# Hybrid decoder layer, last chunk of the input projection: twelve of its sums moved from VectorE to accumulating transfers, whole-weight units removed, and the end of the attention reordered

## The chip, the cores and the metric

The kernel runs on one core of one Trainium2 chip. The metric is the device time of one execution in microseconds (us); lower is better. The core has a matrix engine (TensorE, PE in the profile; PEld is its weight load), VectorE (DVE), ScalarE (ACT), GpSimd (POOL) and SyncE (SP). Each of them works through its own instructions strictly in the order in which the program wrote them, and waits on semaphores where an operand is not ready. Transfers are issued by SP (here: all large weight loads) or by POOL (here: small loads, spills, and whatever adds to its destination), and run on the core's 16 DMA engines, which all queues share.

## What is computed

One decoder layer for one sequence of 256 tokens and 2048 features, in float32. The part that matters:

```python
mod = (c_act @ w_mod + b_mod)[:, None, :]
sh_m, sc_m, g_m, sh_f, sc_f, g_f = jnp.split(mod, 6, axis=-1)
h = rmsnorm(x, mix_pre_w) * (1 + sc_m) + sh_m
proj = h @ w_in
cb, cc, cx, q, k, v, r, a_lr = jnp.split(proj, splits, axis=-1)
y_conv = cb * causal_dwconv3(cc * cx, conv_w)
...
o = gla_chunked(q, k, v, log_a)
o = rmsnorm(o, gla_norm_w) * jax.nn.silu(r)
x = x + g_m * rmsnorm(jnp.concatenate([y_conv, y_gla], -1) @ w_out, mix_post_w)
...
```

`w_in` has 6160 columns: cb, cc and cx with 1024 each, q and k with 512 each, v and r with 1024 each, and 16 for the gate. A second half (the ConvFFN, `w_up` and `w_down`) follows and is not touched.

## The kernel before, in words

**Products in three terms.** A float32 weight tile is loaded by SP, rounded by ScalarE to the faster format (`high`, L139, tile `wh`), and the remainder is formed by VectorE (`low`, L144, tile `wl`). The activations are split likewise. Each 128x128 weight block then takes three matmuls of 256 columns (L574, L575, L576). There are three buffers each for `wh` and `wl`, six for raw weights. A unit that is "plain" (L571) skips rounding and remainder and multiplies the whole float32 weights and activations; each such product shows as two matmul records.

**Chunks.** The modulation vectors are needed before `h` exists, so the 16 blocks of 128 features of `h` are made in four chunks of 2, 4, 5 and 5 blocks (`CHUNKS`), and the input projection runs once over its 48 column tiles for each chunk. The partial sums of a chunk are added into `proj[...]` tiles in SBUF by `evac` (L445 to L457): the first chunk's are copied by ScalarE, each later one added by VectorE (L457, 128x512, one for each pair of column tiles). The last chunk is the subject here. It has 18 units (below: u0 to u17), each of two or three column tiles: u0 to u5 make q, k and v; u6 to u14 make cc, cx and cb in turns; u15 to u17 make r. `FULL = (5, 9, 13)` (L46) makes u5, u9 and u13 plain, of two, three and two column tiles with five blocks each, so 35 products.

**What runs beside it.** The gated linear attention runs between those units: gate (gla_gate0 to 4), then nine levels of score blocks (`gla_level`), each with a difference on VectorE (diff), exponentials on ScalarE (decay), products on VectorE (mult), matmuls (products, L673) and a masked write into the score tile (put; from level 4 on a copy on ScalarE). `gla_v` turns v on TensorE (L662). `gla_out` ends it: `outputs` (L775 to L778) in u15, `norms` (eight squares on ScalarE, L386, a square root, L787, and a reciprocal on VectorE, L788) late in u15, `scaled` (eight scalings on ScalarE, L797) early in u16, then `turn` (L805) and `gate` for the four heads, the first turn late in u17. The convolution runs in four pairs of tiles (`conv_pair`, CONV = u9, u12, u13, u15): c0 is a product on VectorE (L600) and two scalings on ScalarE (L602), c1 in the next unit four fused operations and a product on VectorE (L135, L609) and a rounding on ScalarE (L611), c2 a remainder on VectorE (L615). Two more modulation vectors are summed meanwhile on VectorE, one 128x2048 row block for each step (`macc`, L135). Each such sum starts with a memset and a bias load, both on POOL (L177, L178); the one named f1 below starts early in u8 and is used by VectorE in the same step.

After u17 come the 16 units of the output projection (u18 and on, L841 to L843, matmuls of 512 columns), and then the ConvFFN.

**The order of the work** is written out by hand. `drive` (L74) walks the units; for unit i it emits, in this order: its `early` list, the load and rounding of unit i+2 (`prep`), the remainder of unit i+1 (`low`), its `pre` list, its matmuls, its `mid` list, the `fin` of unit i-1 (that is `evac`), and its `late` list. Each engine's queue is this order, cut down to its own instructions. `hf` tiles (three buffers, `hf_tile`, L420) hold modulated activations; in the last chunk a plain unit reads them until its matmuls are done.

Of the kernel before, what the change touches and what calls it, by code (L numbers as in the profile page):

```python
# [11 lines left out]
ALU = mybir.AluOpType  # L12
# [12 lines left out]
CHUNKS = (2, 4, 5, 5)  # L25
# [16 lines left out]
MODS = (10, 22, 32, 48, 68)  # L42
CHUNK1 = 12
BUSY_TAIL = (15, 16, 17)
F2_AT = (68, 73, 16)
FULL = (5, 9, 13)  # L46
FULL1 = ()
FULL2 = ()
NRAW = 6
# [17 lines left out]
def spread(steps, units):  # L67

    places = [p for u in units for p in (u.early, u.mid)]
    for i, f in enumerate(steps):  # L70
        places[i * len(places) // len(steps)].append(f)
# [31 lines left out]
def layer_kernel(ctx: ExitStack, tc, x, c, w_mod, b_mod, mix_pre_w, mix_post_w, w_in, conv_w, gate_w2, gate_b,  # L103
                 gla_norm_w, w_out, ffn_pre_w, ffn_post_w, w_up, ffn_conv_w, w_down, ident_in, masks_in, out):
    nc = tc.nc
# [12 lines left out]
    def nm(s):  # L118
        uid[0] += 1
        return f"{s}_{uid[0]}"  # L120

    def slot(shape, dt=F32):
        return big.tile(shape, dt, tag="big", name=nm("big"))

    def bank(shape):
        return psp.tile(shape, F32, tag="ps", name=nm("ps"))
# [7 lines left out]
    def stt(o, a, s, b, op0=ALU.mult, op1=ALU.add):  # L134
        nc.vector.scalar_tensor_tensor(o, a, s, b, op0=op0, op1=op1)  # L135
# [24 lines left out]
    def mod_steps(s0, n, a, w, nj, lag=0):  # L160

        accs, cur, rows = [], {}, []

        def use(j, r):
            stt(cur["acc"], r, c_act[:, j:j + 1], cur["acc"])

        def step(j):
            if j >= KT:  # L170
                use(*rows.pop(0))
                return
            if j == 0:
                acc = cur["acc"] = (slot([P, n, w]) if n * w <= 1024 else
                                    wts.tile([P, n, w], F32, tag="macc", name=nm("macc"), bufs=2))
                accs.extend(acc[:, s, :] for s in range(n))
                nc.gpsimd.memset(acc, 0.0)  # L177
                nc.gpsimd.dma_start(acc[0:1, :, :], b_mod_v[:, s0:s0 + n, a:a + w])  # L178
            m = nj if j < KT - nj or nj < 4 else 2
            if j % m == 0:  # L180
                cur["r"] = raw_tile([P, m, n, w])
                if m == 1:
                    nc.sync.dma_start(cur["r"][:, 0, :, :], w_mod_v[:, j, s0:s0 + n, a:a + w])
                else:
                    for s in range(n):
                        nc.sync.dma_start(cur["r"][:, :, s, :], w_mod_v[:, j:j + m, s0 + s, a:a + w])
            rows.append((j, cur["r"][:, j % m, :, :]))
            if j >= lag:
                use(*rows.pop(0))

        return accs, [lambda j=j: step(j) for j in range(KT + lag)]
# [192 lines left out]
    def square_sum(src, dst):  # L384
        jk = wts.tile([P, 512], BF16, tag="junk", name=nm("junk"), bufs=1)
        nc.scalar.activation(jk[:, :src.shape[-1]], src, AF.Square, accum_out=dst)  # L386
# [30 lines left out]
    def act_low(d, src):  # L417
        nc.vector.tensor_sub(d[:, :, 1, :], src, d[:, :, 0, :].bitcast(F32))

    def hf_tile():  # L420
        return wts.tile([P, 2, T], F32, tag="hf", name=nm("hf"), bufs=NHF)
# [23 lines left out]
    def evac(ci, pair, ps):  # L445

        name = names[pair // 2]
        if name not in proj:
            proj[name] = slot([P, 4, T])
        dst = proj[name][:, (pair % 2) * 2:(pair % 2) * 2 + 2, :]  # L450
        if pair not in written:
            written.add(pair)
            nc.scalar.activation(dst, ps, AF.Copy, scale=QS if name == "q" else 1.0)
        elif name == "q":
            stt(dst, ps, QS, dst)
        else:
            nc.vector.tensor_add(dst, dst, ps)  # L457

# [57 lines left out]
    def in_units(ci):  # L516
# [16 lines left out]
        def unit(tiles, plain, by_parts=False):  # L533
# [47 lines left out]
            def fin():  # L581
                for p in dict.fromkeys(nt // 2 for nt in tiles):
                    done[p] = done.get(p, 0) + sum(nt // 2 == p for nt in tiles)
                    if done[p] == 2 and p not in keep:
                        evac(ci, p, banks[p])

            return Unit(prep, lows, mm, [fin])

        return [unit(g, i in (PLAIN, FULL1, FULL2, FULL)[ci], ci == 0 and i == 0) for i, g in enumerate(groups)]

# [169 lines left out]
    def gla_out():  # L760

        st = {}

        def outputs():
            v, s = gla["v"], gla["s"]
            st["ss"] = small.tile([P, 2 * HEADS], F32, tag="gss", name="gss")
            st["ps"] = []
            for t in range(2):
                for g in range(2):
                    ps = bank([P, 2, 256])  # L770
                    for i in range(2):
                        h = g * 2 + i
                        hs = slice(h * 256, (h + 1) * 256)
                        if t == 0:
                            nc.tensor.matmul(ps[:, i, :], s[0][:, h, :], v[0][:, hs], start=True, stop=True)  # L775
                        else:
                            nc.tensor.matmul(ps[:, i, :], s[1][:, h, :], v[0][:, hs], start=True, stop=False)
                            nc.tensor.matmul(ps[:, i, :], s[2][:, h, :], v[1][:, hs], start=False, stop=True)  # L778
                    st["ps"].append(ps)

        def norms():
            ss = st["ss"]
            for t in range(2):
                for h in range(HEADS):
                    square_sum(st["ps"][2 * t + h // 2][:, h % 2, :], ss[:, t * 4 + h:t * 4 + h + 1])
            rs = small.tile([P, 2 * HEADS], F32, tag="grs", name="grs")
            nc.scalar.activation(rs, ss, AF.Sqrt, bias=eps_t, scale=1.0 / 256)  # L787
            nc.vector.reciprocal(rs, rs)  # L788
            st["rs"] = rs

        def scaled():
            rs = st["rs"]
            st["o"] = []
            for t in range(2):
                o = slot([P, 4, 256])
                for h in range(HEADS):
                    nc.scalar.activation(o[:, h, :], st["ps"][2 * t + h // 2][:, h % 2, :], AF.Copy,  # L797
                                         scale=rs[:, t * 4 + h:t * 4 + h + 1])
                st["o"].append(o)

        def turn(e2):
            st[e2] = ps = bank([P, 2, T])
            for i in range(2):
                for t in range(2):
                    nc.tensor.transpose(ps[:, i, t * P:(t + 1) * P], st["o"][t][:, e2, i * P:(i + 1) * P], ident)  # L805

        def gate(e2):
            r = proj[f"r{e2 // 2}"][:, (e2 % 2) * 2:(e2 % 2) * 2 + 2, :]
            for i in range(2):
                stt(r[:, i, :], st[e2][:, i, :], sv[:, 56 + i:57 + i], r[:, i, :], ALU.mult, ALU.mult)  # L810
            mts[4 + e2] = slot([P, 2, 2, T], F32R)
            nc.scalar.copy(mts[4 + e2][:, :, 0, :], r)

        def gate_low(e2):
            r = proj[f"r{e2 // 2}"][:, (e2 % 2) * 2:(e2 % 2) * 2 + 2, :]
            act_low(mts[4 + e2], r)

        return outputs, norms, scaled, turn, gate, gate_low

    def gate_silu(g):  # L820
# [279 lines left out]
    rs = {}  # L1100
# [78 lines left out]
    tail = chunks[-1] + owait  # L1179
# [8 lines left out]
    f1, fsteps = mod_steps(3, 2, 0, 1024, 1)  # L1188
    spread(fsteps, [u for i, u in enumerate(allin) if MODS[3] <= i < MODS[4] and i - ends[2] not in BUSY_TAIL])
    for place, f in seconds:  # L1190
# [27 lines left out]
    outputs, norms, scaled, turn, gate, gate_low = gla_out()  # L1218
    GO = G0 + len(levels) + 3
    tail[GO].early.append(outputs)  # L1220
    tail[GO].late.append(norms)
    tail[GO + 1].early.append(scaled)
    for g in range(2):
        tail[SILU[g]].late.append(lambda g=g: gate_silu(g))
    for e in range(4):
# [3 lines left out]
        tail[GATE[e] - 1].late.append(lambda e=e: turn(e))  # L1229
    for i, u in enumerate(CONV):  # L1230
        c0, c1, c2 = conv_pair(i)
        tail[u].late.append(c0)
        tail[u + 1].pre.append(c1)
        tail[u + 1].late.append(c2)
    owait[8].late.append(warm_sqrt)
    for t in range(2):
        owait[XRE + t].late.append(lambda t=t: load_x(t))
# [152 lines left out]
    f2, fsteps2 = mod_steps(3, 2, 1024, 1024, 1)  # L1390
    spread(fsteps2, allin[F2_AT[0]:F2_AT[1]] + s1[2:F2_AT[2]])
    owait[-1].mid.append(second_norm)
# [57 lines left out]
def build(nc, tc_args=None, arrays=None):  # L1450
    import concourse.tile as _tile

    args = []
    for name, a in arrays.items():
        args.append(nc.dram_tensor(f"in_{name}_dram", a.shape, mybir.dt.from_np(a.dtype), kind="ExternalInput").ap())
    for i, (shape, dtype) in enumerate(_OUTS):
        args.append(nc.dram_tensor(f"out_{i}_dram", shape, getattr(mybir.dt, dtype), kind="ExternalOutput").ap())
    with _tile.TileContext(nc, **(tc_args or {})) as tc:
        with tc.manual_schedule():
            layer_kernel(tc, *args)  # L1460
# [13 lines left out]
```

## Time and profile before

| | |
|---|---|
| time, median of 3 runs | 1219.34 us (1218.43 to 1219.68) |
| the profiled execution's own time | 1219.42 us |
| its span, first to last instruction | 1217.6 us |
| mean granted TensorE clock | 0.995 |
| busy: PE, VectorE, ScalarE, GpSimd | 1180.4, 941.2, 568.4, 33.5 us |
| DMA: queue of SP, queue of POOL | 72.3%, 1.6% of 16 engines' span |
| HBM read | 315.42 MB |

Read it so. The span is what the engines were seen to do; some 1.8 us of the execution lie around it. A busy time says little of what an engine cost: the work has stages with different limits, and what bounds a stage is read from who waits for whom in it. The last chunk's units u3 to u17 lie at about 257 to 356 us of the span, the output projection begins right behind. In the timeline each row is an instruction or a run of like ones: start, duration, engine, line, output and inputs, and in brackets the idle time of the engine before it with what ended it. "Chained" below means the distance from one start to the next on an engine that does not wait; it is a little less than the duration shown, since an instruction's end overlaps the next one's start.

### The profile page before, as it was taken

How to read it: one execution, taken by the hardware profiler on the slowest of the kernel's cores; microseconds unless marked ns; L12 is line 12 of the kernel's file. 1: busy time of each engine (PE TensorE's matmuls, PEld its weight loads, DVE VectorE, ACT ScalarE, POOL GpSimd, SP SyncE). 2: the span in 40 equal slices, each digit the busy share in tenths (PEclk: the TensorE clock that was granted, in tenths of full speed). 3: DMA queues.
4: the chain of work that ended last, by engine and by line, in shares of the span. 5: the costliest groups of instructions: out<-in, count | busy, mean ns of one | idle time of the engine just before them, and what ended most of it. 6: DMA issues, size and time to landing. Idle time of an engine off the chain costs nothing.

```text
span 1217.6 us, 17121 instructions
## 1 busy us (share of the span) xinstructions
PE 1180.4 (97%) x7016; PEld 1041.0 (85%) x7016; DVE 941.2 (77%) x959; ACT 568.4 (47%) x651; POOL 33.5 (3%) x52
## 2 busy tenths in 40 slices
PE   3899999999989999999999999999999999999997
PEld 3899999999977888888888888888888888888885
DVE  6989899899989787984598979698886665444463
ACT  3663333353474437444564545544545543433452
POOL 3000100100000001000000000000000000000000
PEclk9999999999989999999999999999999999999999
DMA  9999899887679996996766766767664665555522
GB/s 343 386 363 390 309 379 396 329 301 243 223 272 375 360 370 230 348 332 217 246 215 240 250 227 235 261 213 269 221 232 151 245 248 184 207 178 202 194 83 69
DMA packets 126622, 320.73 MB, mean 263 GB/s; under 512 B 8309, under 2 KB 34245, under 8 KB 116816
## 3 DMA queue, kind: packets, MB, share of 16 engines
q1 hardware_dynamic: 124048, 312.63, 72.3%
q0 software_dynamic: 2352, 7.00, 1.6%
q8 instruction: 55, 0.90, 0.3%
q14 instruction: 23, 0.19, 0.0%
q10 hardware_dynamic: 144, 0.01, 0.0%
HBM read 315.42 MB, written 4.19 MB: 262 GB/s over the span
## 4 chain that ended last, share of the span: by engine, by line
PE 86%; DVE 7%; DMA 2%; ACT 2%; issue 1%; SPq 0%; DVEq 0%; ACTq 0%
PE ps L985 27%; PE ps L987 14%; PE ps L842 9%; PE ps L843 9%; PE ps L841 9%; PE ps L576 5%; PE ps L574 5%; PE ps L575 5%; DVE macc L135 2%; DVE wl L144 1%; DMA big<-in_w_in_dram 1%; PE ps L314 1%; DVE big L135 1%; DMA big<-in_w_mod_dram 1%; DMA big<-in_x_dram 1%
## 5 line engine op out<-in xcount | busy, mean ns | idle before, releaser
L139 ACT CAST wh<-raw 128x2048 fp32r<-128x2048 f32 (+3 forms) x196 | 361.7, 1848 | 498.7 <-PE ps L985 192.2
L144 DVE TENSOR_TENSOR wl<-raw,wh 128x2048 fp32r<-128x2048 f32 (+3 forms) x196 | 432.5, 2209 | 147.1 <-ACT wh L139 147.1
L985 PE MATMUL ps<-big,wh 128*128 128x512 f32 x1400 | 495.0, 399 | 0.0
L987 PE MATMUL ps<-big,wl 128*128 128x256 f32 x1400 | 392.9, 281 | 0.0
L985 PEld LDWEIGHTS ps<-big,wh 128*128 128x128 f32 x1400 | 263.0, 188 | 65.2
L987 PEld LDWEIGHTS ps<-big,wl 128*128 128x128 f32 x1400 | 264.4, 189 | 0.0
L576 PE MATMUL ps<-big,wl 128*128 128x256 f32 x725 | 205.9, 284 | 4.5 <-DVE wl L144 4.5
L574 PE MATMUL ps<-big,wh 128*128 128x256 f32 x725 | 206.8, 285 | 0.0
L575 PE MATMUL ps<-big,wh 128*128 128x256 f32 x725 | 205.2, 283 | 0.0
L135 DVE SCALAR_TENSOR_TENSOR macc<-raw,c_act,macc 128x2048 f32<-128x2048 f32 (+1 forms) x96 | 199.5, 2078 | 0.9 <-DMA raw<-in_w_mod_dram 0.8
L842 PE MATMUL ps<-wl,big 128*128 128x512 f32 x456 | 178.8, 392 | 3.0 <-DVE wl L144 3.0
L841 PE MATMUL ps<-wh,big 128*128 128x512 f32 x456 | 179.4, 393 | 0.2 <-ACT wh L139 0.2
L843 PE MATMUL ps<-wh,big 128*128 128x512 f32 x456 | 178.6, 392 | 0.0
L576 PEld LDWEIGHTS ps<-big,wl 128*128 128x128 f32 x725 | 138.9, 192 | 6.0 <-DVE wl L144 5.8
L574 PEld LDWEIGHTS ps<-big,wh 128*128 128x128 f32 x725 | 139.0, 192 | 1.7 <-issue 1.3
L575 PEld LDWEIGHTS ps<-big,wh 128*128 128x128 f32 x725 | 139.0, 192 | 0.2
L842 PEld LDWEIGHTS ps<-wl,big 128*128 128x128 f32 x456 | 86.3, 189 | 21.2 <-DVE wl L144 3.3
L841 PEld LDWEIGHTS ps<-wh,big 128*128 128x128 f32 x456 | 86.3, 189 | 18.5 <-ACT wh L139 0.4
L843 PEld LDWEIGHTS ps<-wh,big 128*128 128x128 f32 x456 | 86.3, 189 | 18.2
L135 DVE SCALAR_TENSOR_TENSOR big<-big,fcw,big 128x254 f32<-128x254 f32 (+1 forms) x176 | 72.2, 477 | 0.0
L911 DVE TENSOR_TENSOR big<-big,ps 128x256 f32<-128x256 f32 x88 | 31.2, 416 | 49.2 <-ACT big L909 49.2
L931 ACT ACTIVATE big<-big,fcw 128x256 f32<-128x256 f32 x88 | 37.9, 515 | 11.5 <-DVE big L922 11.5
(213 smaller groups left out, 688.9 us busy)
## 6 DMA issues: line engine op xcount, KB each, us to landing
raw<-in_w_up_dram SPq DMA_DIRECT2D x88, 1024.0 KB, 5.5
raw<-in_w_mod_dram SPq DMA_DIRECT2D x64, 1024.0 KB, 6.2
raw<-in_w_down_dram SPq DMA_DIRECT2D x44, 1024.0 KB, 4.8
raw<-in_w_in_dram SPq DMA_DIRECT2D x28, 960.0 KB, 7.7
raw<-in_w_mod_dram SPq DMA_DIRECT2D x32, 640.0 KB, 7.4
raw<-in_w_out_dram SPq DMA_DIRECT2D x16, 1024.0 KB, 7.5
raw<-in_w_in_dram SPq DMA_DIRECT2D x12, 1024.0 KB, 8.7
raw<-in_w_mod_dram SPq DMA_DIRECT2D x22, 512.0 KB, 8.4
```

The lines of the kernel that those rows point to most:

```text
L135: nc.vector.scalar_tensor_tensor(o, a, s, b, op0=op0, op1=op1)
L139: nc.scalar.copy(hi, raw)
L144: nc.vector.tensor_sub(lo, raw, hi.bitcast(F32))
L574: nc.tensor.matmul(ps, w[0][:, kk, cs], ht[:, k % 2, 0, :], start=st, stop=False)
L575: nc.tensor.matmul(ps, w[0][:, kk, cs], ht[:, k % 2, 1, :], start=False, stop=False)
L576: nc.tensor.matmul(ps, w[1][:, kk, cs], ht[:, k % 2, 0, :], start=False, stop=sp)
L841: nc.tensor.matmul(ps, a[:, i, 0, ts_], w[0][:, kk, ns], start=st, stop=False)
L842: nc.tensor.matmul(ps, a[:, i, 0, ts_], w[1][:, kk, ns], start=False, stop=False)
L843: nc.tensor.matmul(ps, a[:, i, 1, ts_], w[0][:, kk, ns], start=False, stop=sp)
L931: nc.scalar.activation(st["c"][:, o, :], st["u"][o], AF.Copy, scale=fcw[:, 2, ch + o:ch + o + 1])
L985: nc.tensor.matmul(pss[o], wh[:, kk, cs], h2[k // 2][:, k % 2, :, :], start=(first and kk == 0), stop=False)
L987: nc.tensor.matmul(pss[o][:, 1, :], wl[:, kk, cs], h2[k // 2][:, k % 2, 0, :], start=False, stop=(last and kk == 3))
```

## The change

Three edits.

- The sums of cc, cx and v in the last chunk (twelve `evac` calls: four each) no longer run as an addition on VectorE. ScalarE copies the PSUM bank to an `hf` tile, and POOL issues a transfer from that tile to the `proj` tile that adds to its destination. The sums of q, k, cb and r stay on VectorE.
- `FULL` becomes empty: u5, u9 and u13 are multiplied in three terms like the others, so each gets a rounding on ScalarE, a remainder on VectorE, and `wh` and `wl` buffers.
- The end of the attention: the reciprocal moves from `norms` into `scaled`, and `scaled` from the `early` to the `pre` list of u16, that is behind the rounding of u18 on ScalarE and the remainder of u17 on VectorE. Each pair's c0 becomes the first entry of its unit's `late` list (for the last pair: ahead of `norms`). c2 of the last pair moves from u16 to u17.

```diff
+BY_DMA = ("cc", "cx", "v")
 F2_AT = (68, 73, 16)
-FULL = (5, 9, 13)
+FULL = ()
...
         elif name == "q":
             stt(dst, ps, QS, dst)
+        elif ci == len(CHUNKS) - 1 and name[:-1] in BY_DMA:
+            away_sum = hf_tile()
+            nc.scalar.copy(away_sum, ps)
+            nc.gpsimd.dma_start(dst, away_sum, accum_op=ALU.add)
         else:
             nc.vector.tensor_add(dst, dst, ps)
...
             nc.scalar.activation(rs, ss, AF.Sqrt, bias=eps_t, scale=1.0 / 256)
-            nc.vector.reciprocal(rs, rs)
             st["rs"] = rs
 
         def scaled():
             rs = st["rs"]
+            nc.vector.reciprocal(rs, rs)
             st["o"] = []
...
-    tail[GO + 1].early.append(scaled)
+    tail[GO + 1].pre.append(scaled)
...
         c0, c1, c2 = conv_pair(i)
-        tail[u].late.append(c0)
+        tail[u].late.insert(0, c0)
         tail[u + 1].pre.append(c1)
-        tail[u + 1].late.append(c2)
+        tail[u + (1 if i < 3 else 2)].late.append(c2)
```

## The prediction, on record before the run

> **What bounds the kernel now.** I read the page first, for the chain that ended last.
>
> ```profile
> PE 86%; DVE 7%; DMA 2%; ACT 2%; issue 1%; SPq 0%; DVEq 0%; ACTq 0%
> ```
>
> Over the whole kernel TensorE is the bound. The 7% that VectorE holds of the chain must lie in a stage of its own, so I cut out u3 to u17, their end, and what follows.
>
> ```profile
> 252.00:346.50 94.50, 92.60 (x701) 89.25 (x700) 94.16 (x103) 38.87 (x65) 1.10 (x2) 1.00 0.77 260
> 346.50:360.00 13.50, 9.91 (x78) 9.16 (x77) 8.23 (x13) 12.53 (x24) 0.00 (x0) 0.97 0.62 229
> 360.00:366.00 6.00, 6.00 (x15) 4.72 (x16) 6.00 (x5) 2.86 (x3) 0.00 (x0) 0.51 0.74 242
> ```
>
> The columns are the stretch, then busy PE, PEld, DVE, ACT, POOL, granted clock, DMA share and GB/s. In the last chunk VectorE does not rest: 94.16 of 94.50 us, beside TensorE's 92.60. From 346.5 to 360 both have gaps, and then TensorE runs 6 us at a clock of 0.51, which costs about 6.0 x 0.49 = 2.9 us. The timeline shows the two gaps that matter.
>
> ```profile
> 313.47 0.38 PE L673 MATMUL ps<-big 128*128 128x128 f32 x1 [0.96 <-DVE big L457]
> ...
> 359.89 0.80 PE L842 MATMUL ps<-wl,big 128*128 128x512 f32 x1 [2.95 <-DVE wl L144]
> ```
>
> At 313.47 a score product waits until VectorE has emptied a PSUM bank; at 359.89 the output projection (u18) waits for its remainder, which VectorE forms late. So the prize is 2.95 us and, if TensorE's idle time stays short enough, the 2.9 us of the slow clock. Whatever moves the instruction at 359.89 moves everything behind it: from 366 on TensorE is the bound again.
>
> **Whole weights.**
>
> ```profile
> 262.17 0.28 PE L574 MATMUL ps<-big,wh 128*128 128x256 f32 x1
> ...
> 262.53 0.28 PE L574 MATMUL ps<-big,wh 128*128 128x256 f32 x1
> ...
> 267.91 4.48 PE L571 MATMUL ps<-hf,raw 128*128 128x256 f32 x20
> 272.23 1.95 PE L673 MATMUL ps<-big,big 128*128 128x128 f32 x16
> ```
>
> Three terms take 0.36 us from one L574 to the next; ten plain products (20 records) take 4.32, 0.432 each. So 35 products save 35 x 0.072 = 2.5 us on TensorE: 0.72, 1.08 and 0.72 in u5, u9 and u13.
>
> ```profile
> 262.58 1.28 DVE L457 TENSOR_TENSOR big<-big,ps 128x512 f32<-128x512 f32 x2
> 263.78 2.35 DVE L135 SCALAR_TENSOR_TENSOR macc<-raw,c_act,macc 128x2048 f32<-128x2048 f32 x1
> ...
> 274.65 2.15 DVE L144 TENSOR_TENSOR wl<-raw,wh 128x1920 fp32r<-128x1920 f32 x1
> 276.71 1.29 DVE L735 TENSOR_TENSOR big<-big,big 128x512 f32<-128x512 f32 x2
> ...
> 289.37 2.35 DVE L135 SCALAR_TENSOR_TENSOR macc<-raw,c_act,macc 128x2048 f32<-128x2048 f32 x1
> ...
> 317.40 1.49 DVE L144 TENSOR_TENSOR wl<-raw,wh 128x1280 fp32r<-128x1280 f32 x1
> 318.80 1.29 DVE L735 TENSOR_TENSOR big<-big,big 128x512 f32<-128x512 f32 x2
> ```
>
> On VectorE twelve sums go, 0.60 chained each (7.2 us), and three remainders come: 1.40, 2.06 and 1.40 (4.9 us). Net 2.3 us less. Were that all, the end would come about 2.3 sooner. Three things stand against it.
>
> **First: a bias load that queues behind the sums on POOL.** The row at 289.37 is the first step of f1, in u8.
>
> ```profile
> 237.13 1.81 POOL L177 MEMSET macc<- 128x2048 f32 x1
> 239.23 0.51 POOL L178 DMA_DIRECT2D macc<-in_b_mod_dram  x1 [0.29 <-POOL macc L177]
> ```
>
> Before, POOL reached f1's memset 52 us ahead. Now five adding transfers stand before it (four of v, the first of cc), and the fifth waits for ScalarE's copy in u7.
>
> ```profile
> 281.61 0.62 ACT L719 ACTIVATE big<-big 128x512 f32<-128x512 f32 x1
> 290.56 1.78 ACT L139 CAST wh<-raw 128x1920 fp32r<-128x1920 f32 x1
> L453 ACT ACTIVATE big<-ps 128x512 f32<-128x512 f32 x24 | 13.0, 594 | 0.0
> ```
>
> The last exponential of u7 was at 281.61; by then VectorE has lost four sums (2.4) and got one remainder (1.4), so it comes 1.0 earlier, at 280.6. Behind it stand the rounding of u9, which is new (1.78, ends about 282.9), and the copy (0.59): 283.5. POOL issues (0.5), sets memory and issues the bias load 2.10 later (237.13 to 239.23): 286.2. When does that land? For the adding transfers the trace has no row at all; these are its nearest, by KB and us to landing. The two bias loads are the one issued at 239 and the one at 397.
>
> ```profile
> macc<-in_b_mod_dram POOLq DMA_DIRECT2D x1, 8.0 KB, 4.0
> macc<-in_b_mod_dram POOLq DMA_DIRECT2D x1, 8.0 KB, 5.5
> away<-big POOLq DMA_DIRECT2D x4, 512.0 KB, 4.2
> big<-in_mix_post_w_dram POOLq DMA_DIRECT2D x2, 512.0 KB, 9.4
> out_dram<-big SPq DMA_DIRECT2D x8, 256.0 KB, 2.7
> ```
>
> For the bias I take 4.5, ends 4.0 and 5.5: 290.7. VectorE is ready at 289.37 - 5 x 0.60 + 1.40 = 287.8, so it waits 2.9, and its whole queue with it (remainders, score factors, masked writes; TensorE for those). It then is 1.3 late; the new remainder of u9 adds 2.06, one sum less takes 0.6: 2.8 late on the way to c1 of the first pair.
>
> **Second: ScalarE's copies queue behind its rounding in c1.**
>
> ```profile
> 312.85 0.62 ACT L611 CAST big<-big 128x512 fp32r<-128x512 f32 x1 [4.73 <-DVE big L609]
> ...
> 342.64 0.62 ACT L611 CAST big<-big 128x512 fp32r<-128x512 f32 x1 [4.05 <-DVE big L609]
> 343.17 1.26 ACT L139 CAST wh<-raw 128x1280 fp32r<-128x1280 f32 x1
> ```
>
> L611 waits for VectorE, and in u10 and u14 the new copies are emitted behind it. In u10 they empty the bank for which TensorE waited until 313.47: L611 at 312.85 + 2.8 = 315.65, copy 0.53 later and 0.59 long: 316.8, so TensorE is 3.3 us late there. The 1.8 us that u5 and u9 saved are gone. SP's queue is passed by none of this: its loads keep their order, and the raw tiles of u5, u9 and u13 come free sooner, after their remainders. On POOL, mix_post's load moves behind the last adding transfer too; it is read only in u23.
>
> **Third: the reordered end hangs on the last transfer.** From u10 to u14 VectorE loses five sums (3.0) and gains u13's remainder (1.4): 1.2 late at c1 of the third pair. So L611 at 343.8, the copy of the last cx pair done at 343.8 + 0.53 + 0.59 = 344.9, its transfer issued at 345.0. c0 of the last pair needs it, VectorE reaches c0 at about 347.8 (L611 done at 344.4, then c2 0.60, u16's remainder 2.06, cb's sum 0.60, and a hand-over), and c0 now stands ahead of the norms on ScalarE. If the transfer lands L after its issue, c0 starts at 345.1 + L. These rows price the rest:
>
> ```profile
> 344.33 0.38 ACT L386 ACTIVATE junk<-ps 128x256 bf16<-128x256 f32 x1
> ...
> 348.36 1.28 ACT L787 ACT_TABLE_LOAD   x1
> ...
> 350.78 0.91 ACT L602 ACTIVATE big<-big,sv 128x256 f32<-128x256 f32 x2 [0.83 <-DVE big L600]
> 351.60 3.01 ACT L797 ACTIVATE big<-ps,grs 128x256 f32<-128x256 f32 x8
> ```
> ```profile
> 349.99 0.20 DVE L788 RECIPROCAL grs<-grs 128x8 f32<-128x8 f32 x1 [3.34 <-ACT grs L787]
> 350.11 0.64 DVE L600 TENSOR_TENSOR big<-big,big 128x512 f32<-128x512 f32 x1
> ...
> 352.07 1.66 DVE L135 SCALAR_TENSOR_TENSOR big<-big,sv,big 128x255 f32<-128x255 f32 x4
> ...
> 354.37 0.68 DVE L457 TENSOR_TENSOR big<-big,ps 128x512 f32<-128x512 f32 x1
> 356.95 0.69 DVE L615 TENSOR_TENSOR big<-big,big 128x512 fp32r<-128x512 f32 x1 [1.90 <-ACT big L611]
> 357.56 2.28 DVE L144 TENSOR_TENSOR wl<-raw,wh 128x2048 fp32r<-128x2048 f32 x1
> ```
>
> From c0: 0.67 to L602, 0.82 for it, 4.03 for the squares (344.33 to 348.36), 1.63 for table, root and hand-over (to 349.99), 0.12 for the reciprocal, then c1 2.30 and r's sum 0.60, then u18's remainder to TensorE's start 2.33 (357.56 to 359.89): 12.5 us. The wait of 1.90 for L611 drops out, since c2 has moved behind the remainder; VectorE's 3.34 for the root does not, it only moves to u16. The scalings end in time: root done 7.0 after c0, u18's rounding 1.85, five scalings 1.8 make 10.7, less than 12.5. TensorE, even 3.3 late, is through u17 at 355.65 + 3.3 = 359.0. So u18 goes on at 345.1 + L + 12.5 = 357.6 + L, against 359.89.
>
> L lies between 2.7 (256 KB on SP's queue at the end) and 9.4 (512 KB beside full weight loads). An adding transfer of 256 KB reads two operands, beside two weight loads; I take 5.5, between the spill (4.2) and the 9.4. Then 363.1, that is 3.2 late. TensorE's gap is as long as before, so the slow clock stays and cancels. All durations are of the one profiled execution, so the sum is made against its own 1219.42: 1222.6; the median of the runs lies 0.08 below, **1222.5**. From L = 4.5 to 7, 1221.5 to 1224.
>
> The Trainium skill ("DMA: Bandwidth & Descriptors", section on the anatomy of one GpSimd-issued DMA) fits such a transfer with 2.0 us plus bytes over 436e3 per us: 2.6 us for 256 KB, 2.0 for the bias. By that L the sum would be 0.5 late instead of 3.2. The rows above lie over that rule (4.0 and 5.5 for 8 KB), and I go by them. Against the change speaks the Trainium skill's "Collectives: The Full Stack" (section on the bandwidth ceiling): an addition in the DMA engines needs two reads for one write, and so runs at half a copy's rate. No run here shows it yet.
>
> **Rivals.**
> *Short landing* (L up to 4.2, as the spill). VectorE reaches c0 only at 347.8, so u18 is at least 0.5 late and at most 1.9; TensorE's longest idle piece shrinks, and if the clock then stays up, 2.9 come back: 1217 to 1221.3, no change. For it: source and destination are both in SBUF, as the spill's source is. Against: DMA share 0.77 in this stretch.
> *Faster.* The bias lands before VectorE asks, because the copy of u7 comes earlier than I reckon, and L is short: u18 starts 2.9 - 0.5 = 2.4 earlier and the clock stays up, 5.3 together: 1214.1. It decides at a bias in place by 287.8 and L under 3. The page's fit would nearly give this (bias 288.2). Against: both bias rows, and the copy's place behind a new rounding.
> *Crowding.* L of 8 to 9.4, as mix_post's load: the three hf tiles then also hold up ScalarE's copies in u11, and u18 is 5.7 to 7.1 late: 1225 to 1226.5.
>
> **How the numbers follow.** Forecast 0.42; short landing 0.28; faster 0.18; crowding 0.12. About 0.2% (2.4 us) is what a measurement of this kernel can tell from no change. Slower takes the forecast and crowding, 0.54; same 0.28; faster 0.18. The range of 8 in 10 leaves out most of the faster case and the upper end of crowding: 1216 to 1226.5. The forecast's own range is 1221.5 to 1224.
>
> **What would show it.** Right: POOL's memset L177 near 284 instead of 237; a VectorE wait of 2 to 4 us on a bias transfer at the macc step near 288; TensorE waiting on ScalarE's copy near 316; c0 of the last pair (L600) waiting on an adding transfer near 350, and the root near 357 with VectorE idle before it; a slow clock again behind u18's start. Wrong: adding transfers that land under 4 us, a bias that is there in time, or u18 starting before 359.9 at a full clock.

## The result, and the profile after

The changed kernel takes 1225.54 us (median of 6 runs, 1224.91 to 1225.95), the kernel before 1219.09 beside it (6 runs, 1218.43 to 1219.68): a ratio of 1.0053, 95% interval 1.0040 to 1.0066, so 6.4 us slower. Its profiled execution took 1225.3 us with a span of 1223.5, which is 5.9 over the profiled execution of before. The forecast was slower by 3.2, at 1222.5: right in its direction and in the places it named, half the size. The time lies inside the wide range (1216 to 1226.5), but outside the forecast's own, 1221.5 to 1224; it lies where the rival called crowding was put.

The chain that ended last, on the page of the changed kernel:

```profile
PE 85%; DMA 4%; issue 4%; DVE 4%; ACT 1%; POOL 0%; SPq 0%; DVEq 0%; ACTq 0%; POOLq 0%
```

VectorE's share has gone from 7% to 4%, and transfers and "issue" have come in its place. The stretches (columns as before: PE, PEld, DVE, ACT, POOL, granted clock, DMA share, GB/s):

```profile
252.00:346.50 94.50, 87.94 (x694) 86.53 (x693) 88.08 (x90) 44.92 (x69) 11.97 (x13) 0.96 0.87 272
346.50:360.00 13.50, 13.50 (x115) 13.50 (x114) 6.38 (x7) 7.13 (x22) 1.96 (x3) 1.00 0.88 315
360.00:366.00 6.00, 1.81 (x8) 1.13 (x7) 4.61 (x8) 5.99 (x12) 0.00 (x0) 0.82 0.34 137
366.00:372.00 6.00, 5.66 (x16) 4.26 (x16) 6.00 (x6) 5.97 (x6) 0.00 (x0) 0.61 0.56 188
```

VectorE, which hardly rested in the last chunk before (94.16 of 94.50), now is busy for 88.08: two waits, of 4.32 and 1.64 us, fall into this stretch (their rows are below). TensorE's hole, which lay between 346.5 and 360, has moved behind 360, where it works 1.81 of 6 us. The timeline has the steps. POOL's rows:

```profile
283.91 0.85 POOL L460 DMA_DIRECT2D big<-hf  x1 [7.01 <-ACT hf L459]
284.44 2.13 POOL L178 MEMSET macc<- 128x2048 f32 x1
286.88 0.55 POOL L179 DMA_DIRECT2D macc<-in_b_mod_dram  x1 [0.30 <-POOL macc L178]
...
323.77 1.74 POOL L460 DMA_DIRECT2D big<-hf  x2 [3.29 <-ACT hf L459]
...
348.90 0.86 POOL L460 DMA_DIRECT2D big<-hf  x1 [7.16 <-ACT hf L459]
```

VectorE's rows, with the bracket telling how long it sat idle and what ended that ("issue" stands where the profile shows no releaser; the bias transfer issued at 286.88 took 5.5 us to land, that is until 292.4):

```profile
292.42 2.35 DVE L136 SCALAR_TENSOR_TENSOR macc<-raw,c_act,macc 128x2048 f32<-128x2048 f32 x1 [4.32 <-issue]
...
332.73 0.69 DVE L605 TENSOR_TENSOR big<-big,big 128x512 f32<-128x512 f32 x1 [1.64 <-DMA big<-hf]
...
354.17 0.69 DVE L605 TENSOR_TENSOR big<-big,big 128x512 f32<-128x512 f32 x1 [2.66 <-DMA big<-hf]
...
361.36 0.20 DVE L797 RECIPROCAL grs<-grs 128x8 f32<-128x8 f32 x1 [5.10 <-ACT grs L792]
```

Four waits: for f1's bias in u8, for an adding transfer at c0 of the second pair, for the last adding transfer at c0 of the last pair, and for the square root that stands behind that c0 on ScalarE. TensorE's rows:

```profile
298.19 2.98 PE L678 MATMUL ps<-big 128*128 128x128 f32 x16 [3.07 <-DVE big L740]
...
318.51 1.18 PE L678 MATMUL ps<-big 128*128 128x128 f32 x8 [2.22 <-ACT hf L459]
...
363.90 0.47 PE L810 MATMUL ps<-ident,big 128*128 128x128 f32 x1 [3.57 <-ACT big L802]
...
366.67 0.80 PE L847 MATMUL ps<-wl,big 128*128 128x512 f32 x1 [0.34 <-DVE wl L145]
```

The output projection's second product starts at 366.67 instead of 359.89, 6.78 later. Less of the slow clock lies over the products of u18 than before: then they ran slowly from 359.89 until about 365.9, now from 366.67 until about 370.7. That is 2 us less at half speed, which gives back about 0.9 to 1.0, and 6.78 - 0.9 = 5.9 is the whole difference of the profiled executions. So everything to explain lies ahead of that one instruction.

### The profile page after: what moved, and what is told of

It reads as the page before. It is cut to its first block, busy times and chain, and to the rows that moved or that the text cites. A ratio compares the mean times of both kernels' runs of the same rounds, so it can differ in the third digit from the quotient of the medians.

```text
span 1223.5 us, 17251 instructions
## 1 busy us (share of the span) xinstructions
PE 1181.0 (97%) x7051; PEld 1043.6 (85%) x7051; DVE 939.0 (77%) x950; ACT 578.0 (47%) x666; POOL 44.7 (4%) x64
## 4 chain that ended last, share of the span: by engine, by line
PE 85%; DMA 4%; issue 4%; DVE 4%; ACT 1%; POOL 0%; SPq 0%; DVEq 0%; ACTq 0%; POOLq 0%
PE ps L990 27%; PE ps L992 14%; PE ps L848 9%; PE ps L847 9%; PE ps L846 9%; PE ps L581 5%; PE ps L579 5%; PE ps L580 5%; DMA raw<-in_w_mod_dram 2%; DMA big<-hf 1%; DVE macc L136 1%; DVE wl L145 1%; PE ps L315 1%; DMA big<-in_w_mod_dram 1%; DVE big L136 1%
## 5 line engine op out<-in xcount | busy, mean ns | idle before, releaser
L140 ACT CAST wh<-raw 128x2048 fp32r<-128x2048 f32 (+3 forms) x199 | 366.0, 1841 | 499.9 <-PE ps L990 192.1
L145 DVE TENSOR_TENSOR wl<-raw,wh 128x2048 fp32r<-128x2048 f32 (+3 forms) x199 | 437.3, 2200 | 144.4 <-ACT wh L140 144.4
L992 PE MATMUL ps<-big,wl 128*128 128x256 f32 x1400 | 392.9, 281 | 0.0
L990 PEld LDWEIGHTS ps<-big,wh 128*128 128x128 f32 x1400 | 263.1, 188 | 65.0
L992 PEld LDWEIGHTS ps<-big,wl 128*128 128x128 f32 x1400 | 264.4, 189 | 0.0
L581 PE MATMUL ps<-big,wl 128*128 128x256 f32 x760 | 216.6, 285 | 4.2 <-DVE wl L145 4.2
L579 PE MATMUL ps<-big,wh 128*128 128x256 f32 x760 | 218.0, 287 | 0.0
L580 PE MATMUL ps<-big,wh 128*128 128x256 f32 x760 | 216.0, 284 | 0.0
L581 PEld LDWEIGHTS ps<-big,wl 128*128 128x128 f32 x760 | 146.7, 193 | 5.5 <-DVE wl L145 5.5
L579 PEld LDWEIGHTS ps<-big,wh 128*128 128x128 f32 x760 | 146.8, 193 | 1.6 <-issue 1.3
L580 PEld LDWEIGHTS ps<-big,wh 128*128 128x128 f32 x760 | 146.9, 193 | 0.2
```

The costliest lines, as they stand in the source:

```text
L140: nc.scalar.copy(hi, raw)
L145: nc.vector.tensor_sub(lo, raw, hi.bitcast(F32))
L579: nc.tensor.matmul(ps, w[0][:, kk, cs], ht[:, k % 2, 0, :], start=st, stop=False)
L580: nc.tensor.matmul(ps, w[0][:, kk, cs], ht[:, k % 2, 1, :], start=False, stop=False)
L581: nc.tensor.matmul(ps, w[1][:, kk, cs], ht[:, k % 2, 0, :], start=False, stop=sp)
L990: nc.tensor.matmul(pss[o], wh[:, kk, cs], h2[k // 2][:, k % 2, :, :], start=(first and kk == 0), stop=False)
```

## The experiments

My theory after these rows: the sums taken from VectorE are worth what was reckoned, but three waits on POOL's transfers (the bias behind the adding transfers; two c0 on adding transfers, the last with the norms behind it) give back more. The rivals: transfers that crowd the DMA queues wherever they stand; the missing whole weights; the new order itself. Each ratio below is to the kernel before on the same chip, with its 95% interval.

**The bias load early.**

```diff
+    f1_begin = []
+    f1, fsteps = mod_steps(3, 2, 0, 1024, 1, 0, f1_begin)
...
+    tail[3].late.append(f1_begin[0])
```

`f1_begin[0]` is f1's memset and bias load; the additions stay where they were.

> The changed kernel with one thing moved: f1's memset and bias load are given to POOL's queue in u3, ahead of all adding transfers. Theory (VectorE is made late by the bias that lands at 292.4, then by c0 on its last transfer): the wait of 4.32 us at the macc step disappears, all that VectorE does behind it in u9 to u17 comes about 4 us sooner, ScalarE's copies and so the adding transfers with it, and u18's second product moves from 366.7 to about 362.5; c0 of the last pair still waits 2 to 3 us for its transfer. Time 1220 to 1222, some 4 to 5 under the changed kernel. Rival 1 (twelve adding transfers crowd the DMA queues, so weights and landings are late wherever the bias stands): within 1 us of 1225.5. Rival 2 (the price is the missing whole weights, that is the three new remainders and roundings): the wait goes but the lateness stays, 1224 to 1225.5.

1221.26 us, ratio 1.0020 (1.0011 to 1.0028). VectorE's waits from 255 to 372 (total, times, longest):

```profile
DVE grs L803 <- ACT grs L798: 5.1, 1, 5.1
DVE big L611 <- DMA big<-hf: 4.5, 2, 2.8
DVE big L626 <- ACT big L622: 0.7, 1, 0.7
```
```profile
362.45 0.80 PE L853 MATMUL ps<-wl,big 128*128 128x512 f32 x1 [0.35 <-DVE wl L145]
```

The macc wait is gone from the list, the two on adding transfers are still there, and u18 starts 4.2 earlier, for a wait that was 4.3. One queue position on POOL was worth 4 us. Crowding and missing whole weights both said that the time would hardly move.

**The norms ahead of the last pair's c0.**

```diff
-        tail[u].late.insert(0, c0)
+        tail[u].late.insert(0 if i < 3 else len(tail[u].late), c0)
```

> The changed kernel with c0 of the last pair alone back behind the norms on ScalarE's and VectorE's order; the bias still lands late. Theory (the end hangs on the last transfer, since the norms stand behind a c0 that waits for it): the squares start right after the last copy near 348.6 and the root is done near 354 instead of 361; c0 finds its transfer landed (354.1) and the chain to u18 gets shorter by about 5 us: 1218 to 1221. The macc wait of 4.3 stays. Rival 1 (crowding): the last landing does not move, nor does u18 by more than 1: 1225. Rival 2 (missing whole weights): root earlier, but VectorE has as much work ahead of u18's remainder as before: 1223 to 1225.

1219.29 us, ratio 1.0005 (0.9996 to 1.0014), 5.9 under the changed kernel by the ratios.

```profile
292.31 2.35 DVE L136 SCALAR_TENSOR_TENSOR macc<-raw,c_act,macc 128x2048 f32<-128x2048 f32 x1 [4.23 <-issue]
...
354.29 0.69 DVE L605 TENSOR_TENSOR big<-big,big 128x512 f32<-128x512 f32 x1 [2.93 <-DMA big<-hf]
...
361.62 0.50 PE L847 MATMUL ps<-wl,big 128*128 128x512 f32 x1 [0.76 <-DVE wl L145]
```

c0 still waits for its transfer, to 354.29; I had it find the transfer landed, and that was wrong. But the squares now run beside that wait instead of behind it, VectorE's wait for the root is gone, and u18 starts 5.05 earlier. Behind its gap of 0.76 the granted clock stays at 1.00 from 360 to 372, so the slow clock is gone as well.

**Both.** The two edits together.

> Both moves together: bias load early, norms ahead of the last pair's c0. Theory: the two waits stand one behind the other on VectorE's way to u18, so their gains add, about 4 and 5 us, until TensorE itself is the bound in u17; u18's gap shrinks to below 1 us and the slow clock behind it may go: 1212 to 1217, under the kernel before. Rival 1 (crowding): 1224 to 1226. Rival 2 (missing whole weights): 1219 to 1224, not under the kernel before.

1214.27 us, ratio 0.9965 (0.9953 to 0.9978): faster than the kernel before, with all twelve transfers in place.

```profile
349.82 0.69 DVE L611 TENSOR_TENSOR big<-big,big 128x512 f32<-128x512 f32 x1 [3.03 <-DMA big<-hf]
...
357.14 0.50 PE L853 MATMUL ps<-wl,big 128*128 128x512 f32 x1 [0.86 <-DVE wl L145]
```

From 1.0053 the early bias takes 0.0033, the norms 0.0048, both 0.0088: within the intervals the two add, as two waits in one row do. Crowding is out as the price of this change, since the twelve transfers are still issued (the last still takes 5.6 us to land).

**The new order alone.** The kernel before with the third edit only.

```diff
+BY_DMA = ()
 F2_AT = (68, 73, 16)
 FULL = (5, 9, 13)
```

> The kernel before with the new order of attention's end alone: reciprocal with the scaling, c0 ahead of everything in its unit, c2 of the last pair one unit later; whole weights and VectorE's own sums are kept, no adding transfer. Theory: without a transfer to wait for, c0 in front costs only its own 0.64 and 0.82 us ahead of the norms, and c2 moved late takes the 1.90 us wait for L611 out of the way: 1217 to 1219.5, not slower than before. Rival 3 (the new order is the price by itself, the root comes late because c0 and its ScalarE step stand ahead of it): 1221 to 1224.

1217.69 us, ratio 0.9992 (0.9983 to 1.0000): at most 2 us faster, and no gain that counts.

```profile
354.28 0.20 DVE L797 RECIPROCAL grs<-grs 128x8 f32<-128x8 f32 x1 [5.09 <-ACT grs L792]
...
359.60 0.80 PE L847 MATMUL ps<-wl,big 128*128 128x512 f32 x1 [0.90 <-DVE wl L145]
```

Without a transfer the reordered end costs nothing by itself: u18 starts at 359.60, before at 359.89, and this execution stands 0.7 later from its macc step of u4 on (261.01 against 260.32). TensorE's idling is not gone but split: 1.14 and 0.77 us in front of the turns, 0.90 in front of u18, and 3.4 us of slow clock still follow. And VectorE waits 5.09 for the root instead of 3.34: c0 in front, with its step on ScalarE, pushes the squares back even here.

**Whole weights removed alone.** The kernel before with `FULL = ()`.

> The kernel before with its whole weights left out alone (u5, u9 and u13 multiply in three terms); VectorE keeps its twelve sums, no transfer, the old order. Theory (VectorE sets the last chunk's pace): TensorE's 2.5 us saved count for nothing, the three remainders of 1.40, 2.06 and 1.40 stand on VectorE's way to u18, so it starts up to 4.9 later than 359.9: some 4 to 5 over the kernel before of the same call. Rival (TensorE is the bound there and VectorE has room): 2.5 under it to no change.

1223.49 us, ratio 1.0037 (1.0025 to 1.0050), about 4.5 slower.

```profile
364.78 0.80 PE L842 MATMUL ps<-wl,big 128*128 128x512 f32 x1 [2.95 <-DVE wl L144]
```

u18 is 4.89 late with the same wait of 2.95 in front of it. The three remainders, reckoned at 4.9, come through whole; TensorE's saving counts for nothing in this kernel, where VectorE sets the pace.

**Plain transfers instead of adding ones.**

```diff
-            nc.gpsimd.dma_start(dst, away_sum, accum_op=ALU.add)
+            nc.gpsimd.dma_start(dst, away_sum)
```

> The changed kernel with transfers that overwrite instead of adding, which leaves the earlier chunks' sums of cc, cx and v out of the result; queues, sizes and times of issue are the same. If it is the addition (two reads for one write) that makes the landings long (7.4 us in the middle, 5.3 for the last), they fall to 3 to 4 us, the two waits of c0 on a transfer (1.64 and 2.66) go, and the time falls by about 4 to 1221 to 1222. If the landing is set by the queues and by the weights' loads beside it, the landings stay within 1 us of those of the changed kernel and so does the time, 1224.5 to 1226.

1222.43 us, ratio 1.0025 (1.0015 to 1.0036); the profiled execution took 1220.22, so its rows show the kernel in one of its better runs. It fits neither expectation. DMA issues from 255 to 352, first of the changed kernel, then of this one (KB each, median us to landing):

```profile
big<-hf POOLq DMA_DIRECT2D x12, 256.0 KB, 7.4
```
```profile
big<-hf POOLq DMA_DIRECT2D x12, 256.0 KB, 6.3
```

The median falls by 1.1, not by half. Where less else is moving it falls by about two fifths: the transfer issued at 291.7 took 3.9 us adding and 2.3 plain (DMA share of the 4 us behind it, with the adding one: 0.67), the pair at 318.6 4.2 and 2.4 (median). Where the share is 1.02 to 1.03, it is 8.9 against 7.4 (the pair at 265) and 9.6 against 6.9 (the pair at 323.7). From issue to issue the adding transfer of 256 KB took 0.5 to 3.3 us longer than the plain one. How much of that is the addition itself is not settled, since the traffic beside is not quite the same in the two executions; most of a landing of 7 to 10 us is there without it. On VectorE the second pair's wait disappears and the last pair's shrinks:

```profile
350.62 0.69 DVE L605 TENSOR_TENSOR big<-big,big 128x512 f32<-128x512 f32 x1 [0.98 <-DMA big<-hf]
```

POOL's queue over the whole span (packets, MB, share of 16 engines), of the kernel before, the changed one and this one:

```profile
q0 software_dynamic: 2352, 7.00, 1.6%
```
```profile
q0 software_dynamic: 4080, 10.15, 3.1%
```
```profile
q0 software_dynamic: 3312, 10.15, 2.3%
```

The same 3.15 MB take 1728 packets and 1.5% of the engines when they add, 960 packets and 0.7% when they don't. It fits what the Trainium skill says of the addition in a ReduceScatter ("Collectives: The Full Stack", section on the bandwidth ceiling): two reads for one write, so half a copy's rate. Here it is 1.8 times the packets and about twice the time on the engines.

**The old order, with transfers.** The changed kernel with its third edit undone.

> The changed kernel with its third edit undone: adding transfers and no whole weights, but reciprocal, c0 and c2 in the places of the kernel before. Theory: the bias still lands late (wait of 4.2 to 4.4 at the macc step), but no norm stands behind a c0 that waits for a transfer; from the last rounding of c1 (347.5) the old end takes 17.25 us to u18 (342.64 to 359.89), so u18 starts near 364.7 instead of 366.7: 1222.5 to 1224.5. Rival (the new order is good also with transfers): 1227 or more, since the wait of 1.90 for the rounding of c2 comes back and the wait for the transfer stays.

1224.70 us, ratio 1.0045 (1.0032 to 1.0057), just over what I expected and not to be told from the changed kernel's 1.0053. The same macc step of u4 in the changed kernel and in this one, then the rows of the end:

```profile
260.49 2.34 DVE L136 SCALAR_TENSOR_TENSOR macc<-raw,c_act,macc 128x2048 f32<-128x2048 f32 x1
```
```profile
261.53 2.35 DVE L136 SCALAR_TENSOR_TENSOR macc<-raw,c_act,macc 128x2048 f32<-128x2048 f32 x1
...
349.16 0.62 ACT L616 CAST big<-big 128x512 fp32r<-128x512 f32 x1 [4.04 <-DVE big L614]
...
366.93 0.50 PE L847 MATMUL ps<-wl,big 128*128 128x512 f32 x1 [2.95 <-DVE wl L145]
```

This execution stands 1.04 later from before the last chunk on. Less that, u18 starts at 365.9, 0.8 before the changed kernel and not 2: the rounding at 349.16 is at 348.1 (347.50 there), and from it the end takes 17.8, not the 17.25 of the kernel before. So with transfers, too, the reordering as a whole neither costs nor brings anything that shows.

**The order without c0 in front, no transfers.** The kernel before, with the reciprocal moved into `scaled`, `scaled` moved, and c2 of the last pair late.

```diff
...
-    tail[GO + 1].early.append(scaled)
+    tail[GO + 1].pre.append(scaled)
...
         tail[u].late.append(c0)
         tail[u + 1].pre.append(c1)
-        tail[u + 1].late.append(c2)
+        tail[u + (1 if i < 3 else 2)].late.append(c2)
```

> The kernel before with two thirds of the new order: reciprocal with the scaling and c2 of the last pair one unit later, but c0 stays at its unit's end behind the norms. No transfers, whole weights kept. Theory (c0 in front costs 1.5 us ahead of the root in the last pair, the other two help): the wait of 1.90 for the rounding and part of the wait for the root go, u18 starts 2 to 3 sooner, its gap falls under 1 us and the slow clock (2.9) goes with it: 4 to 6 under the kernel before of the same call. Rival (the order as a whole is worth the 0.8 measured with c0 in front): within 1.5 of it.

1213.05 us, ratio 0.9950 (0.9936 to 0.9963): 6.1 faster than the kernel before.

```profile
350.21 0.20 DVE L797 RECIPROCAL grs<-grs 128x8 f32<-128x8 f32 x1 [1.35 <-ACT grs L792]
```
```profile
355.87 0.50 PE L847 MATMUL ps<-wl,big 128*128 128x512 f32 x1
```

No wait stands in front of u18, so no slow clock follows. The third edit held the whole prize of the kernel before (the wait of 2.95 and 2.9 of slow clock); its one line for c0 gave it away again (0.9992 with that line, 0.9950 without).

**Four versions on the way to better.** With the bias early: the last sum of cc and of cx (pairs 7 and 11) back on VectorE; c0 at its unit's end in all four pairs; the two sums of u10 (pairs 5 and 6) on VectorE; and c0 at the end with pairs 5, 6 and 11 on VectorE. The sums come back by one condition, here that of the last of the four:

```diff
-        elif ci == len(CHUNKS) - 1 and name[:-1] in BY_DMA:
+        elif ci == len(CHUNKS) - 1 and name[:-1] in BY_DMA and pair not in (5, 6, 11):
```

> The kernel with the bias early and the last pair's norms ahead of c0 (1214.3), in which VectorE now also adds the last sum of cc and the last of cx itself (ten transfers instead of twelve). Theory (VectorE's way sets u18's start, and the last transfer still holds it up 3.03 us at c0): that wait goes, two sums (1.2) come, VectorE is up to 1.8 earlier, and u18 gains what is left of its wait for VectorE, 0.86 at most: 0.5 to 1 under that kernel, a ratio of about 0.996 to the kernel before. Rival (what is left is crowding by transfers): no change from 0.9965.

0.9968 (0.9956 to 0.9981), 1214.27 us. c0's wait for the last transfer is gone (one of 1.3 us for the root comes in its place), and u18 starts without waiting, 0.64 earlier; the time cannot tell it from 0.9965.

```profile
356.50 0.50 PE L853 MATMUL ps<-wl,big 128*128 128x512 f32 x1
```

> The kernel with the bias early and c0 at its unit's end in all four pairs, not in the last alone; all twelve transfers. Theory: the wait of 1.62 us of the second pair's c0 for its transfer goes (other work stands ahead of c0), and no other wait comes in its place: VectorE 1.6 earlier, of which u18 can use 0.86: a ratio of 0.9955 to 0.9965. Rival (c0 in front is needed by ScalarE's two scalings, which c1 waits for): VectorE waits for them at c1, 1 to 2 slower, 0.9975.

0.9969 (0.9958 to 0.9980), 1214.78 us: a miss. The second pair's c0 waits as before; at its unit's end, too, VectorE reaches it before the transfer has landed:

```profile
328.84 0.69 DVE L611 TENSOR_TENSOR big<-big,big 128x512 f32<-128x512 f32 x1 [1.91 <-DMA big<-hf]
```

> The kernel with the bias early and the last pair's norms ahead of c0, in which VectorE adds the two sums emitted in u10, those whose copies stand behind ScalarE's rounding and keep TensorE waiting 2.22 us (and then slow for some 3.4). Theory A (TensorE's own lateness in u10 to u17 is hidden, VectorE alone sets u18): the wait and the slow clock at 313 to 317 go, yet two more sums (1.2) on VectorE make u18 0 to 1.2 later: ratio 0.9965 to 0.9975. Theory B (the wait behind ScalarE's copy costs by itself, as the prediction said): TensorE is 3 to 4 us earlier and the time falls by 1 to 3: 0.994 to 0.9955.

0.9959 (0.9946 to 0.9971), 1213.57 us: between the two theories, with an interval that reaches into both, and both had the wait wrong. It does not go; TensorE waits for VectorE's sum instead of ScalarE's copy, and its clock is still slow behind it.

```profile
313.70 1.65 PE L684 MATMUL ps<-big 128*128 128x128 f32 x6 [1.68 <-DVE big L468]
```

> Everything found so far together: bias early, c0 at its unit's end in all pairs, and three sums back on VectorE (the two of u10 and the last of cx, whose transfer c0 of the last pair waits for); nine transfers are left, none of which anybody should wait for. Theory: VectorE loses the waits of 1.62 and 3.03 and takes three sums (1.8), 2.8 earlier; TensorE loses the wait of 2.22 and the slow clock at 313 to 317; u18 starts 2 to 3 before 357.1: a ratio of about 0.994, as the kernel with whole weights and late c2 (0.995) or 1 us under it. Rival (transfers crowd whatever is done): 0.9965.

0.9957 (0.9944 to 0.9971), 1213.21 us. u18 starts at 356.02 with no wait, beside 355.87 in the kernel with whole weights and late c2. The stretch from 300 to 330 shows a likely reason why the two meet there, first of this kernel, then of that one:

```profile
300.00:330.00 30.00, 27.52 (x219) 27.16 (x219) 29.93 (x37) 14.16 (x32) 1.74 (x2) 0.94 0.72 221
```
```profile
300.00:330.00 30.00, 28.34 (x210) 26.95 (x209) 29.93 (x38) 12.25 (x29) 0.00 (x0) 1.00 0.72 248
```

TensorE has 2.5 us less work in this kernel by the reckoning, but is idle for 2.48 instead of 1.66 here and loses some 1.8 (30 x 0.06) to a slow clock, 2.6 together. So about what the removed whole weights save goes into two waits (0.80 and 1.68 us) and the slow clock behind them. Whether these can be removed without new ones was not tried; 0.9957 and 0.9950 cannot be told apart.

## Why the prediction was right, and where it fell short

**Whole weights and sums.** The remainders alone made u18 4.89 late (4.9 reckoned), and VectorE's busy time fell by 2.2 (941.2 to 939.0; 2.3 reckoned for sums and remainders together). No run takes the twelve sums away alone.

**First, the bias.** The mechanism was right: memset at 284.44, a wait at the macc step near 288. Its size was not: 4.32 instead of 2.9. VectorE was ready at 292.42 - 4.32 = 288.1 (287.8 reckoned); the landing came at 292.4 instead of 290.7, because the fifth adding issue began at 283.91 (283.5 reckoned), the bias load was issued 2.44 behind the start of the memset (2.10), and the bias took 5.5 to land (4.5). The 0.5 between that issue and the memset held (0.53), though the issue itself shows as 0.85. The upper of the two bias rows would have been the right one. Moving the load early confirmed 4 us of price. By the Trainium skill's fit ("DMA: Bandwidth & Descriptors", section on the anatomy of one GpSimd-issued DMA) the bias would have taken 2.0 us and an adding transfer 2.6. The trace has 5.5, and 3.3 to 10.3; only the plain transfers at 291.9 (2.3) and 318.6 (2.4) come near that fit.

**Second, the copies in u10.** TensorE waited at 318.51 for the copy, 2.22 us, where I had 316.8; the 1.7 between them is the first term's error carried on. Behind it, and behind the 3.07 us at 298.19 that the bias wait caused, the granted clock fell to half for 3.4 us each, which I had not reckoned. All that was hidden, though: in the changed kernel TensorE is idle for 3.57 us ahead of u18, and u18 waits for the end that hangs on c0.

**Third, the end.** Here is the step that failed: "From u10 to u14 VectorE loses five sums (3.0) and gains u13's remainder (1.4): 1.2 late at c1 of the third pair. So L611 at 343.8." That rounding came at 347.50, 3.7 later.

```profile
347.50 0.62 ACT L616 CAST big<-big 128x512 fp32r<-128x512 f32 x1 [3.94 <-DVE big L614]
```

Of this 1.7 is the bias, and 1.64 a wait that I put at nothing without a reason: c0 of the second pair also waited for an adding transfer. By the times it is the first of the two that POOL issued from 323.77 on, which took 8.9 us to land, until 332.7, where that c0 starts. I had asked that question of the last pair alone. The other 0.3 to 0.4 stays open. From there on the reckoning held to a few tenths: the last transfer issued 1.4 behind the rounding (1.2 reckoned), its landing 5.2 (5.5 taken), and from c0 at 354.17 to u18 at 366.67 12.5 us, as worked out. 3.7 + 0.2 - 0.3 makes the 3.6 between 363.1 and 366.67.

**The slow clock.** The claim was that it stays and cancels. It was as long as before (6.8 us), but less of it lay over u18's products, which gave back 0.9.

**The rivals.** A short landing did not come: 5.2 for the last. (Its lower bound, 0.5 late, is 0.4 by its own terms: 347.8 + 12.5 - 359.9. Nothing hangs on it.) Crowding gave the right number, 1225 to 1226.5, by the wrong way: it put 8 to 9.4 us on the last landing, which took 5.2. A landing of that length came in the second pair and cost 1.64, and with the same twelve transfers and two things moved the kernel is 4.3 faster than before. The faster rival named a bias in time and a last landing under 3 us as its condition. With the bias in time and the norms no longer behind the landing its 1214.1 was measured (1214.27), but with a landing of 5.6; that the numbers agree is chance.

## What to carry to other kernels

Work handed to a transfer does not only free an engine: its issue takes a place in a queue, and the small load behind it may be the one that someone needs. Before sums go to an adding transfer, list every reader of each destination and what stands behind that reader on its engine; a reader that waits belongs behind independent work, not ahead of it. And an edit in three parts is worth measuring in three: here one line out of one part kept back a gain of 6.1 us that needs no transfer at all.

## What the runs showed of the hardware

An adding transfer of 256 KB from SBUF to SBUF took 3.3 to 10.3 us to land beside the weights' loads, and POOL 0.85 us to issue (2.3 to 7.5 and 0.54 for the same transfer without addition).

TensorE's granted clock fell to half behind some idle stretches and not behind others, for about 3.4 or 6.8 us. It was halved for 3.4 us behind 2.22 us of idling with 0.80 a little ahead of it (both edits together), behind 1.68 with 0.79 ahead (u10's sums on VectorE), and behind 1.14, 0.77 and 0.90 close together (the new order alone). It was halved for 6.8 behind 2.22 with 1.76 ahead (plain transfers), and behind 2.95 in the kernel before. But the same 2.95 in the old order with transfers brought 3.4, which began only 1.5 us after the stretch had ended, and 2.74 at 298 with plain transfers brought none. None came either behind 0.96 and 0.58 some 13 us apart (the kernel with whole weights and late c2), nor behind 0.86 and 0.76. So what counts here is not the length of one stretch alone, and these runs give no threshold.
